# Reordering the stages of a diffusion trunk: the first gate products and all chunk inverses go ahead of the query pass, and those gates' weights are split by ScalarE and GpSimd

## The chip, the cores and the metric

The kernel runs on one core of a Trainium2 chip. The metric is device time in microseconds (us) of one execution. Engines are named as the profile names them: PE (TensorE matmul), DVE (VectorE), ACT (ScalarE), POOL (GpSimd), SP (SyncE, which here issues most DMAs).

## The reference

One layer of a trunk over 2048 latent tokens and 256 context tokens, model width 1024. The tokens are normalised and modulated (`h`), and one wide input projection feeds two mixers and their gates:

```
qkv, beta, decay, k_att, v_att = split(h @ w_state)
za, q_att, zb, ga, gb          = split(h @ w_rest)
q, k, v = l2norm/silu(short_conv5(qkv))             # 4 heads of 128
oa = delta_rule(q, k, v, g, beta)  +  the same backwards in time
ob = windowed attention(q_att, k_att, v_att, sink)   # 8 heads of 64
y  = sigmoid(ga) * (norm(oa)*silu(za) @ w_proj_a) + sigmoid(gb) * (ob*silu(zb) @ w_proj_b)
out = x + gate * (y @ w_out)
```

The delta rule runs in chunks. For each chunk, head and direction a unit lower triangular matrix is inverted, `t_mat = solve(I + a_mat)`, where `a_mat` is made of that chunk's keys, decays and betas alone; queries don't enter it. The inverses are then used by a scan over the chunks, which carries a state forwards and one backwards, and which needs the queries for its outputs. The gate products `za, zb, ga, gb` (3072 columns) depend on `h` alone.

## The kernel before

All matrices are fp32, and each large product is made of three: an operand is split into a high part rounded to fp32r and a low part (`wh`, `wl` for weights, `hh`, `hl` for the tokens), and high x high, low x high and high x low are summed. So each block of weights first costs two elementwise steps: a rounding copy (`wh <- wr`, L242, on POOL) and a subtraction (`wl <- wr, wh`, L243, on DVE), both in `weights` at L235. `fm_dense` (L520) then makes 24 products of 128 x 512 for each 128 columns and each group of 512 tokens.

The stages, in the order in which the program is written:

1. Modulation, normalised tokens `hh0..hh3` (four groups of 512 tokens) and the context `hh4`, attention keys and values.
2. Keys and values of the delta rule (`qkv(ORDER, ...)`, L678): products `lps`, copied to a tile `y` by ACT (L633), a convolution over five tokens on DVE (L562, L564), transposes and chunk products on PE (`zt` L594, `gps` L603 and L617), and the results stored to DRAM: the chunk matrices to `Nsp`, the betas to `brT` (L543, in `scalars2`).
3. The query pass (L700): `qkv([0, 1, 2, 3])` for the delta rule's queries, and between its groups `q_block` for the attention's queries (products `tmps`, 256 columns wide, L365 to L367).
4. The first gates (L837): all 24 blocks of 128 gate columns for token groups 2 and 3 (`rps`, 1152 products), each followed by a tanh on ACT (L809) and, for the first 8 blocks, a DVE product (L811). Beside them runs `mod_gate`, whose sums `gacc` are made on POOL (L223).
5. The inverses. `base` (L719) inverts 128 triangular matrices at once, one to a partition, by 62 steps of two DVE products each (L746, L748); it is called for two sets of chunks. `base4` (L763) does the last 32 matrices, each spread over four partitions: it reloads `N` from `Nsp`, scales it (L778, L779), copies it to the other partitions by DMA (L783), makes 63 pairs of products (L788, L790) and stores `X4sp` by 16 DMAs (L795).
6. The scan, with the gates of groups 1 and 0 between its steps; then attention, output projections, and the last product.

The scheduler of the framework reorders instructions of each engine within the bounds of their dependences, by a priority that follows the written order; what results is shown below where it matters. On one engine instructions then run strictly in that order, and an instruction that waits holds up all behind it.

Memory is taken from pools. A pool that is opened after another was closed on the same side gets the same SBUF addresses, and its tiles wait, tile by tile, for the last use of what lay there. Before, the pools of stages 2 and 3 for `y`, `cacc` and their like (`p1y`, `p1b`) are one pair that stays open through both; they are closed before the gates, and `base2` (which holds the second set's `N`, and `btmp`, `nb` and the tiles of `base4`) is opened in their place. It stays open to the end of the scan. Of the sum buffers that `lps`, `tmps` and `rps` share (`acc`), there are three.

Of the kernel before, what the change touches and what calls it, by code (L numbers as in the profile page):

```python
# [7 lines left out]
F32 = mybir.dt.float32  # L8
F32R = mybir.dt.float32r
BF16 = mybir.dt.bfloat16  # L10
AF = mybir.ActivationFunctionType
ALU = mybir.AluOpType
# [5 lines left out]
KT = D // 128  # L18
NB, NCB = L // 128, LC // 128
NC = NB + NCB  # L20
H = 4
EPS = 1e-6
C_ST, C_QB = 1536, 2320
# [5 lines left out]
def f32(ap):  # L29
    return ap.bitcast(F32)  # L30
# [10 lines left out]
def _hybrid(ctx, tc, nc, V, S, G, T, ins, out, dbg, upto):  # L41
    dma = nc.sync.dma_start
# [8 lines left out]
    def mem(tag):  # L51
        if dbg is not None:
            print("MEM", tag, tile.free_sbuf_bytes_per_partition(tc))
# [11 lines left out]
    w_in = ins["w_in"][0]  # L65
# [166 lines left out]
            dma(gsp[:, n * 512:n * 512 + 512], grow)  # L232
            yield

    def weights(src, kt):  # L235

        wh = wq.tile([128, KT, 128], F32R, name="wh")
        wl = wq.tile([128, KT, 128], F32R, name="wl")
        for k in range(0, kt, 4):
            wr = wq.tile([128, 4, 128], F32, name="wr", bufs=2)  # L240
            dma(wr, src[k * 128:(k + 4) * 128].rearrange("(k p) c -> p k c", p=128))
            G.tensor_scalar(wh[:, k:k + 4], wr, 1.0, 1.0, op0=ALU.mult, op1=ALU.mult)  # L242
            V.tensor_tensor(wl[:, k:k + 4], wr, f32(wh[:, k:k + 4]), op=ALU.subtract)  # L243
        return wh, wl

    ORDER = [8, 9, 10, 11, 4, 5, 6, 7]
# [2 lines left out]
    if True:  # L249
# [48 lines left out]
        for j in range(2):  # L298
            mps = [psum("acc" if n == 0 else "hps", [4, 512], name=f"mps{n}") for n in range(2)]
            for k in range(KT):  # L300
# [10 lines left out]
                if j == 0 and 2 <= k < 2 + NCB:  # L311
                    c = k - 2
# [48 lines left out]
        def tm_dense(c, wh, wl, n):  # L361
            ps = acc([128, 512], name="tmps")
            xh, xl = hsrc(c)
            for k in range(KT):
                T.matmul(ps[:, :n], lhsT=xh[:, k], rhs=wh[:, k], start=k == 0, stop=False)  # L365
                T.matmul(ps[:, :n], lhsT=xl[:, k], rhs=wh[:, k], start=False, stop=False)
                T.matmul(ps[:, :n], lhsT=xh[:, k], rhs=wl[:, k], start=False, stop=k == KT - 1)  # L367
            return ps[:, :n]

        with tc.issue_after(wm_dma.ins):  # L370
            wh, wl = tm_weights(C_ST, NST)
# [4 lines left out]
        def norm_w(pool, nm):  # L376

            wn = pool.tile([128, 2, 64], F32, name="wn", bufs=1)
            with tc.issue_after(wm_dma.ins):
                dma(wn[:, 0], ins[nm].to_broadcast([128, 64]))  # L380
            x, y = (wn[:, j].rearrange("p (a h f) -> p a h f", a=2, h=2) for j in range(2))
            G.tensor_copy(y[:, :, 0], x[:, :, 1])
            G.tensor_copy(y[:, :, 1], x[:, :, 0])
            return wn

        wn = norm_w(pa, "k_norm_w")
# [81 lines left out]
        def q_block(pool, c, hv, ps, wn):  # L468
            y = qk_norm_rope(pool, 2, ps, 4, c, wn)
            qh = pb.tile([128, 4, 2, 64], F32R, name="qh", tag="st")  # L470
            S.copy(qh[:, :, 0], y)
            V.tensor_tensor(qh[:, :, 1], y, f32(qh[:, :, 0]), op=ALU.subtract)
            kt = psum("zt", [128, 4, 128], F32R)
            for h in range(4):
                T.transpose(kt[:, h], qh[:, h].rearrange("p x d -> p (x d)"), identr)
            qs = pb.tile([128, 4, 128], F32, name="qs", tag="o")
            S.copy(qs, f32(kt))
            adma(Qsp[c - NCB, :, hv * 4:hv * 4 + 4], qs)
# [3 lines left out]
        for gi in range(8):  # L482
            xts = []
            for j in range(2):
                c = NCB + gi * 2 + j
# [5 lines left out]
            if gi == 7:  # L491
                px_.__exit__(None, None, None)
                wq_ = tc.tile_pool(name="wts", bufs=2, reuse_waits="tile")
                wq = wq_.__enter__()
            c = NCB + gi * 2
# [125 lines left out]

    def qkv(order, after, w=None, beside=()):
        w = w or weights(w_in[:, order[0] * 128:order[0] * 128 + 128], KT)
        beside = iter(beside)
        for mi, m in enumerate(order):
            segs = [(hh[4], hl[4], 0, LC)] if m >= 4 else []
            segs += [(hh[gi], hl[gi], NCB + gi * 4, 512) for gi in range(4)]
            ys = []
            for si, (xh, xl, c0, n) in enumerate(segs):
                ps = acc([128, 512], name="lps")[:, :n]  # L630
                fm_dense(ps, w, xh, xl)
                y = py.tile([128, 516], F32, name="y", bufs=4)
                S.copy(y[:, 2:2 + n], ps)  # L633
                if c0 <= NCB:
                    V.memset(y[:, 0:2], 0.0)
                else:
                    V.tensor_copy(y[:, 0:2], ys[-1][0][:, 512:514])
                    V.tensor_copy(ys[-1][0][:, 514:516], y[:, 2:4])
                if c0 == 0 or c0 == NCB + 12:
                    V.memset(y[:, n + 2:n + 4], 0.0)  # L640
                ys.append((y, c0, n))
                if si == 1:
                    nxt = order[mi + 1] if mi + 1 < len(order) else after
                    wnext = None if nxt is None else weights(w_in[:, nxt * 128:nxt * 128 + 128], KT)
                if si == len(segs) - 1:
                    w = wnext
                    done = [ys[-2], ys[-1]]
                elif c0 > NCB or c0 == 0:
                    done = [ys[-1 if c0 == 0 else -2]]
                else:  # L650
                    done = []
                for y_, c_, n_ in done:
                    finish(m, conv(y_, m, n_), c_, n_)
                next(beside, None)
            if 4 <= m < 8:
                sk = ssk[:, :, m % 4]
                G.tensor_scalar(sk, sk, 4 * EPS, 1.0, op0=ALU.add, op1=ALU.mult)
                V.reciprocal(rk2[:, :, m % 4], sk)
                rsq(rin[:, :, m % 4], sk, 1)
            if m < 4:  # L660
                aq = alpha[:, :, m]
                G.tensor_scalar(aq, aq, 4 * EPS, 1.0, op0=ALU.add, op1=ALU.mult)
                rsq(aq, aq)
                G.tensor_scalar(aq, aq, 0.5 * 128 ** -0.5, 1.0, op0=ALU.mult, op1=ALU.mult)
# [16 lines left out]
    dc_.__exit__(None, None, None)  # L681
    hpools.pop().__exit__(None, None, None)

    def q_pass(pool):
        wn = norm_w(pool, "q_norm_w")
        for hv in range(2):
            wh = pool.tile([128, KT, 256], F32R, name="qwh", bufs=1)
            wl = pool.tile([128, KT, 256], F32R, name="qwl", bufs=1)
            col = C_QB + hv * 256
            for k in range(0, KT, 2):  # L690
                wr = wq.tile([128, 2, 256], F32, name="wrq", tag="wr")
                dma(wr, w_in[k * 128:(k + 2) * 128, col:col + 256].rearrange("(k p) c -> p k c", p=128))
                G.tensor_scalar(wh[:, k:k + 2], wr, 1.0, 1.0, op0=ALU.mult, op1=ALU.mult)
                V.tensor_tensor(wl[:, k:k + 2], wr, f32(wh[:, k:k + 2]), op=ALU.subtract)
            for c in range(NCB, NC):
                q_block(pool, c, hv, tm_dense(c, wh, wl, 256), wn)
                if c % 2 == 1:
                    yield

    with tc.tile_pool(name="q_pass", bufs=2, side="right", reuse_waits="tile") as pq:  # L700
        jobs = q_pass(pq)
        qkv([0, 1, 2, 3], None, None, jobs)
        for _ in jobs:
            pass
    bs_ = tc.tile_pool(name="base", bufs=1, side="right", reuse_waits="tile")
    bs = bs_.__enter__()

# [86 lines left out]
                    p0 = q * 32 + d * 16 + ci * 8  # L794
                    dma(X4sp[d, ci, q], X[p0:p0 + 8])  # L795

    def rest(ev, m, groups):

        col, dst, mm = ((C_ZA, zasp, m) if m < 4 else (C_ZB, zbsp, m - 4) if m < 8 else
                        (C_GA, gasp, m - 8) if m < 16 else (C_GB, gbsp, m - 16))  # L800
        w = weights(w_in[:, col + mm * 128:col + mm * 128 + 128], KT)
        return w, dst, mm

    def rest_run(ev, job, m, gi):
# [10 lines left out]
    PACE = -1  # L815
    NWO = 5
    LAT = lambda *cs: [NCB + c for c in cs]
    mem("p1b q")
    pb_.__exit__(None, None, None)
    py_.__exit__(None, None, None)  # L820
    psum_phase("right", mg0=1, mg1=1, og=1, gd0=1, gd1=1)

    def gates(ms, gis, beside=()):
        beside = iter(beside)
        job = rest(ev, ms[0], None)
        for i, m in enumerate(ms):
            for j, gi in enumerate(gis):
                rest_run(ev, job, m, gi)
                if j == 0:
                    nxt = rest(ev, ms[i + 1], None) if i + 1 < len(ms) else None  # L830
                    next(beside, None)
            job = nxt

    bs2_ = tc.tile_pool(name="base2", bufs=1, reuse_waits="tile")
    bs2 = bs2_.__enter__()
    with tc.tile_pool(name="gate", bufs=1, reuse_waits="tile") as gp:
        gates(list(range(24)), (2, 3), mod_gate(gp, ones))  # L837
    LAST = (LAT(14, 15), LAT(0, 1))
    for si, (fr, bk, np_) in enumerate((([0, 1] + LAT(*range(0, 6)), [0, 1] + LAT(*range(10, 16)), bs),
                                        (LAT(*range(6, 14)), LAT(*range(2, 10)), bs2))):  # L840
# [2 lines left out]
                pass  # L843
    base4(*LAST)
    mem("r1a")
    bs_.__exit__(None, None, None)
    hpools.pop().__exit__(None, None, None)
    hpools.pop().__exit__(None, None, None)

# [292 lines left out]
    with tc.tile_pool(name="scan", bufs=1, side="right", reuse_waits="tile") as scp:  # L1142
# [6 lines left out]
        gates(list(range(4, BESIDE)), (1, 0))  # L1149
        mem("r1b")  # L1150
        scl_.__exit__(None, None, None)
    bs2_.__exit__(None, None, None)


    def proj_w():
# [193 lines left out]
```

## Time and profile before

| | us |
|---|---|
| three runs | 2044.96, 2047.9, 2050.6 (median 2047.9) |
| the profiled execution | 2046.15 |
| its span, first to last instruction | 2044.3 |
| PE busy in the span | 1966.8 (96%) |
| DVE busy | 1421.5 (70%) |
| ACT busy | 760.4 (37%) |
| POOL busy | 742.9 (36%) |

Times in a trace are us from the start of the span. Matmuls overlap their neighbours, so a matmul is listed with 0.40 us and yet starts 0.23 us after the one before it; idle PE in a window is its length less the busy time. `PEclk` is the share of the full clock that PE was granted. In a row of instruction groups stand the line, the engine, the operation, output and inputs, their sizes, the count, the total busy time, the mean in ns, and the idle time of the engine before them with what ended it.

### The profile page before, as it was taken

How to read it: one execution, taken by the hardware profiler on the slowest of the kernel's cores; microseconds unless marked ns; L12 is line 12 of the kernel's file. 1: busy time of each engine (PE TensorE's matmuls, PEld its weight loads, DVE VectorE, ACT ScalarE, POOL GpSimd, SP SyncE). 2: the span in 40 equal slices, each digit the busy share in tenths (PEclk: the TensorE clock that was granted, in tenths of full speed). 3: DMA queues.
4: the chain of work that ended last, by engine and by line, in shares of the span. 5: the costliest groups of instructions: out<-in, count | busy, mean ns of one | idle time of the engine just before them, and what ended most of it. 6: DMA issues, size and time to landing. Idle time of an engine off the chain costs nothing. (4 is left out here: it accounts for less than half of the span.)

```text
span 2044.3 us, 32068 instructions
## 1 busy us (share of the span) xinstructions
PE 1966.8 (96%) x11043; PEld 1643.2 (80%) x11043; DVE 1421.5 (70%) x2715; ACT 760.4 (37%) x1927; POOL 742.9 (36%) x876
## 2 busy tenths in 40 slices
PE   6899999989999999999999999999989999999999
PEld 3888888778898677787788888878868888878887
DVE  6888766667766999999689655536577777753322
ACT  5655555544443211101122233325476556531100
POOL 2862211235553433224322234324256443442321
PEclk8999999999999999999999999999999999999999
DMA  7462236754447533437876787663456655355542
GB/s 256 141 166 85 89 97 165 188 149 155 147 136 197 154 109 111 132 98 220 201 218 205 221 244 214 185 207 116 129 165 204 185 167 158 120 174 189 185 144 93
DMA packets 375511, 333.12 MB, mean 163 GB/s; under 512 B 83832, under 2 KB 299184, under 8 KB 374708
## 3 DMA queue, kind: packets, MB, share of 16 engines
q1 hardware_dynamic: 347924, 288.59, 49.1%
q10 hardware_dynamic: 27424, 42.48, 5.9%
q8 instruction: 87, 1.43, 0.3%
q14 instruction: 76, 0.62, 0.1%
HBM read 220.28 MB, written 109.13 MB: 161 GB/s over the span
## 5 line engine op out<-in xcount | busy, mean ns | idle before, releaser
L523 PE MATMUL rps<-hh,wh 128*128 128x512 f32 x768 | 309.9, 404 | 10.1 <-DVE rt L811 5.2
L525 PE MATMUL rps<-hh,wl 128*128 128x512 f32 x768 | 310.3, 404 | 1.6 <-DVE wl L243 1.6
L524 PE MATMUL rps<-hl,wh 128*128 128x512 f32 x768 | 307.8, 401 | 0.0
L242 POOL TENSOR_SCALAR wh<-wr 128x512 fp32r<-128x512 f32 x120 | 104.7, 885 | 278.6 <-PE rps L524 105.8
L523 PEld LDWEIGHTS rps<-hh,wh 128*128 128x128 f32 x768 | 145.6, 190 | 47.1 <-POOL wh L242 4.9
L525 PEld LDWEIGHTS rps<-hh,wl 128*128 128x128 f32 x768 | 145.4, 189 | 35.1 <-DVE wl L243 2.4
L523 PE MATMUL lps<-hh,wh 128*128 128x512 f32 (+1 forms) x448 | 172.1, 384 | 0.3 <-ACT y L633 0.3
L524 PEld LDWEIGHTS rps<-hl,wh 128*128 128x128 f32 x768 | 145.8, 190 | 32.9
L525 PE MATMUL lps<-hh,wl 128*128 128x512 f32 (+1 forms) x448 | 171.1, 382 | 0.0
L524 PE MATMUL lps<-hl,wh 128*128 128x512 f32 (+1 forms) x448 | 171.1, 382 | 0.0
L562 DVE SCALAR_TENSOR_TENSOR cacc<-y,cw,cacc 128x512 f32<-128x512 f32 (+1 forms) x224 | 160.6, 739 | 14.3 <-ACT cacc L560 11.3
L809 ACT ACTIVATE rt<-rps 128x512 f32<-128x512 f32 x96 | 57.3, 597 | 287.5 <-PE rps L525 228.6
L909 DVE CUSTOM_DVE_ANT_0 pr<-sc,band,sk 128x640 f32<-128x640 f32 (+1 forms) x128 | 106.4, 863 | 42.5 <-PE sc L905 22.1
L937 DVE TENSOR_TENSOR pl<-pt,ph 128x512 fp32r<-128x512 f32 x156 | 105.0, 685 | 40.9 <-ACT ph L935 40.3
L935 ACT CAST ph<-pt 128x512 fp32r<-128x512 f32 x156 | 90.2, 585 | 111.7 <-PE pt L933 77.0
L748 DVE TENSOR_TENSOR N<-N,btmp 128x62 f32<-128x62 f32 (+30 forms) x124 | 123.7, 997 | 3.1
L746 DVE TENSOR_TENSOR btmp<-N 128x62 f32<-128x62 f32 (+30 forms) x124 | 119.2, 962 | 3.2
L919 POOL TENSOR_SCALAR pr<-pr,sm 128x640 f32<-128x640 f32 (+1 forms) x128 | 98.9, 793 | 57.1 <-DVE sm L917 44.5
L911 ACT ACTIVATE pr<-pr,sm 128x640 f32<-128x640 f32 (+1 forms) x128 | 104.0, 815 | 24.6 <-DVE sm L909 24.6
L1198 PE MATMUL pps<-yh,wph 128*128 128x512 f32 x256 | 105.1, 414 | 5.0 <-DVE tb L1206 2.0
L243 DVE TENSOR_TENSOR wl<-wr,wh 128x512 fp32r<-128x512 f32 x120 | 94.0, 796 | 18.1 <-POOL wh L242 17.9
L1199 PE MATMUL pps<-yl,wph 128*128 128x512 f32 x256 | 101.7, 397 | 0.9 <-DVE yl L1181 0.9
(301 smaller groups left out, 4925.9 us busy)
## 6 DMA issues: line engine op xcount, KB each, us to landing
wr<-in_w_in_dram SPq DMA_DIRECT2D x120, 256.0 KB
kw<-Ksp SPq DMA_DIRECT2D x28, 384.0 KB
x<-vsp SPq DMA_DIRECT2D x36, 256.0 KB
k<-ksp SPq DMA_DIRECT2D x34, 256.0 KB
kT<-kTsp SPq DMA_DIRECT2D x34, 256.0 KB
wm<-in_w_mod_dram SPq DMA_DIRECT2D x16, 512.0 KB
xt<-in_x_dram SPq DMA_DIRECT2D x16, 512.0 KB
dtl<-Dsp SPq DMA_DIRECT2D x32, 256.0 KB
```

Source lines behind the costliest of these rows:

```text
L242: G.tensor_scalar(wh[:, k:k + 4], wr, 1.0, 1.0, op0=ALU.mult, op1=ALU.mult)
L523: T.matmul(ps, lhsT=wh[:, k], rhs=xh[:, k], start=k == 0, stop=False)
L524: T.matmul(ps, lhsT=wh[:, k], rhs=xl[:, k], start=False, stop=False)
L525: T.matmul(ps, lhsT=wl[:, k], rhs=xh[:, k], start=False, stop=k == kt - 1)
L562: V.scalar_tensor_tensor(a, y[:, t:t + n], cw[:, m, t:t + 1], a, op0=ALU.mult, op1=ALU.add)
L746: V.tensor_tensor(tv, A[:, m + 1:, m].unsqueeze(2).to_broadcast([h1 + n, r, m]), A[:, m, 0:m].unsqueeze(1).to_broadcast([h1 + n, r, m]), o ...
L748: V.tensor_tensor(A[:, m + 1:, 0:m], A[:, m + 1:, 0:m], tv, op=ALU.add)
L909: V.tensor_tensor_reduce(s_, ps[:, o:768], band[:, b0:b0 + W + 256], -0.125, sk[:, 1, hd:hd + 1], ALU.add, ALU.min, sm[:, h, 1:2])
L911: S.activation(s_, s_, AF.Exp, scale=-1.0, bias=sm[:, h, 1:2], accum_out=sm[:, h, 2:3])
L937: V.tensor_tensor(pl, pt, f32(ph), op=ALU.subtract)
L1198: T.matmul(ps, lhsT=wh[:, k, ms], rhs=hs[k], start=k == 0, stop=False)
L1199: T.matmul(ps, lhsT=wh[:, k, ms], rhs=ls[k], start=False, stop=False)
```

## The change

Stage 4 and all of stage 5 move ahead of stage 3: keys and values, then gates and inverses, then the query pass, then the scan. For these gates alone the weights are split by ACT (the rounding copy, `S.copy`) and POOL (the subtraction) in place of POOL and DVE. Pools and banks follow: `p1y` and `p1b` are closed after the keys and values, `base2` takes their place; it is closed when the inverses are written down, and a second pair `q1y`, `q1b` is opened at the same addresses for the query pass. Lines of the changed kernel are numbered otherwise: the subtraction for these gates is L244, base's products L729 and L731, base4's L771 and L773, its scaling L761 and L762, its stores L778, the copy to `y` L637.

```diff
-    def weights(src, kt):
+    def weights(src, kt, beside_base=False):
...
-            G.tensor_scalar(wh[:, k:k + 4], wr, 1.0, 1.0, op0=ALU.mult, op1=ALU.mult)
-            V.tensor_tensor(wl[:, k:k + 4], wr, f32(wh[:, k:k + 4]), op=ALU.subtract)
+            if beside_base:
+                S.copy(wh[:, k:k + 4], wr)
+                G.tensor_tensor(wl[:, k:k + 4], wr, f32(wh[:, k:k + 4]), op=ALU.subtract)
+            else:
+                G.tensor_scalar(wh[:, k:k + 4], wr, 1.0, 1.0, op0=ALU.mult, op1=ALU.mult)
+                V.tensor_tensor(wl[:, k:k + 4], wr, f32(wh[:, k:k + 4]), op=ALU.subtract)
...
-    def q_pass(pool):
...
-    with tc.tile_pool(name="q_pass", bufs=2, side="right", reuse_waits="tile") as pq:
-        jobs = q_pass(pq)
-        qkv([0, 1, 2, 3], None, None, jobs)
-        for _ in jobs:
-            pass
     bs_ = tc.tile_pool(name="base", bufs=1, side="right", reuse_waits="tile")
...
-    psum_phase("right", mg0=1, mg1=1, og=1, gd0=1, gd1=1)
+    psum_phase("right")
+    psum_phase("right", gd0=1, gd1=1)
...
-        gates(list(range(24)), (2, 3), mod_gate(gp, ones))
+        gates(list(range(24)), (2, 3), mod_gate(gp, ones), True)
...
     base4(*LAST)
     mem("r1a")
+    bs2_.__exit__(None, None, None)
     bs_.__exit__(None, None, None)
+
+    def q_pass(pool):
...
+    psum_phase("right")
+    psum_phase("right", zt=3, gps=2)
+    py_ = tc.tile_pool(name="q1y", bufs=2, reuse_waits="tile")
+    py = py_.__enter__()
+    pb_ = tc.tile_pool(name="q1b", bufs=2, reuse_waits="tile")
+    pb = pb_.__enter__()
+    with tc.tile_pool(name="q_pass", bufs=2, side="right", reuse_waits="tile") as pq:
+        jobs = q_pass(pq)
+        qkv([0, 1, 2, 3], None, None, jobs)
+        for _ in jobs:
+            pass
...
+    psum_phase("right", mg0=1, mg1=1, og=1, gd0=1, gd1=1)
     hpools.pop().__exit__(None, None, None)
     hpools.pop().__exit__(None, None, None)
...
         scl_.__exit__(None, None, None)
-    bs2_.__exit__(None, None, None)
```

What this makes of the order on two engines. First DVE around `base4`, whose pairs of products write `btmp`. Before, these are its rows a little after the pairs begin; the names other than `N` and `btmp` are the scan's and the gates' (in brackets stand the semaphores that a row waits for; DMAHW are those of DMAs):

```order
L788 TENSOR_TENSOR btmp<-N,btmp 128x61 [waits DVE_49]
L790 TENSOR_TENSOR btmp<-btmp 128x61 [waits DVE_49]
L1120 TENSOR_TENSOR oa_10579<-ops,oa_10579 128x512 [waits PE_49]
L788 TENSOR_TENSOR btmp<-N,btmp 128x60 [waits DVE_49]
L1076 TENSOR_TENSOR v_10609<-vps,brs 128x512 [waits PE_49]
L790 TENSOR_TENSOR btmp<-btmp 128x60 [waits DVE_49]
L1076 TENSOR_TENSOR v_10647<-vps,brs 128x512 [waits PE_49]
L788 TENSOR_TENSOR btmp<-N,btmp 128x118 [waits DVE_49]
L243 TENSOR_TENSOR wl<-wr,wh 128x512 [waits DMAHW3_49,PE_49,Pool_49]
```

In the changed kernel the pairs of `base4` stand in one block of 126 rows with nothing between them. This is the block's end and what follows it, the first `y` of the query pass:

```order
L771 TENSOR_TENSOR btmp<-N,btmp 128x32 [waits DVE_49]
L773 TENSOR_TENSOR btmp<-btmp 128x32 [waits DVE_49]
L771 TENSOR_TENSOR btmp<-N,btmp 128x16 [waits DVE_49]
L773 TENSOR_TENSOR btmp<-btmp 128x16 [waits DVE_49]
L639 MEMSET y 128x2 [waits DMAHW4_49,DMAHW3_49,DMAHW5_49,DMAHW2_49,DMAHW6_49,DMAHW1_49,DMAHW7_49,DMAHW0_49,DVE_49]
L641 COPY y<-y 128x2 [waits Activation_49]
L476 TENSOR_TENSOR qh<-xn,qh 128x4x64 [waits Activation_49] x2
L402 TENSOR_TENSOR xn<-tmps,ssn 128x256 [waits DVE_49,PE_49]
```

`base4` stood among the scan's work before and now stands alone between the second set of inverses and the query pass, whose first memset of `y` waits for DVE itself and for all eight DMA semaphores.

Second ACT at the head of the query pass. Before, with the tail of the keys and values (`junk`, `st`, `pt`) around the first `sq` and `y` of the queries:

```order
L392 ACTIVATE sq<-tmps 128x256 [waits PE_49]
L560 ACTIVATE cacc<-y,cw 128x512 [waits DMAHW6_49]
L600 ACTIVATE junk,ssk<-zt 128x128 [waits PE_49,Activation_49]
L600 ACTIVATE junk,ssk<-zt 128x128 [waits Activation_49] x2
L633 COPY y<-lps 128x512 [waits DVE_49,PE_49]
L600 ACTIVATE junk,ssk<-zt 128x128 [waits Activation_49]
L612 COPY st<-zt 128x512 [waits DMAHW4_49]
```

In the changed kernel, from the last tanh of the gates (`rt`) on:

```order
L792 ACTIVATE rt<-rps 128x512 [waits DMAHW2_49,PE_49]
L795 DMA gbsp_132<-rt 128x512 [waits Activation_49]
L396 ACTIVATE sq<-tmps 128x256 [waits PE_49]
L396 ACTIVATE sq<-tmps 128x256 [waits DVE_49,PE_49] x2
L637 COPY y<-lps 128x512 [waits DMAHW3_49,DMAHW4_49,DMAHW2_49,DMAHW5_49,DMAHW1_49,DMAHW6_49,DMAHW0_49,DMAHW7_49,DVE_49,Pool_49]
L475 CAST qh<-xn 128x4x64 x2
L637 COPY y<-lps 128x512
L564 ACTIVATE cacc<-y,cw 128x512 [waits DVE_49,Activation_49] x2
```

The copy of the first `lps` to `y` waited for PE and DVE. Now PE is covered by the `sq` ahead of it, and the copy waits for DVE, for POOL and for DMAs on all eight semaphores. The DMAs that stand last in those eight, in SP's order, are the second eight stores of `X4sp` (L778).

More of the change, by code (lines that the diff above doesn't have):

```diff
@@ L682, in _hybrid @@
     hpools.pop().__exit__(None, None, None)
-    def q_pass(pool):
[L685 to L698, printed above, removed]
-    with tc.tile_pool(name="q_pass", bufs=2, side="right", reuse_waits="tile") as pq:
-        jobs = q_pass(pq)
-        qkv([0, 1, 2, 3], None, None, jobs)
-        for _ in jobs:
-            pass
     bs_ = tc.tile_pool(name="base", bufs=1, side="right", reuse_waits="tile")
@@ L795, in base4, with rest @@
                     dma(X4sp[d, ci, q], X[p0:p0 + 8])
-    def rest(ev, m, groups):
+    def rest(ev, m, beside_base):
         col, dst, mm = ((C_ZA, zasp, m) if m < 4 else (C_ZB, zbsp, m - 4) if m < 8 else
                         (C_GA, gasp, m - 8) if m < 16 else (C_GB, gbsp, m - 16))
-        w = weights(w_in[:, col + mm * 128:col + mm * 128 + 128], KT)
+        w = weights(w_in[:, col + mm * 128:col + mm * 128 + 128], KT, beside_base)
         return w, dst, mm
@@ L817, in _hybrid, with gates @@
     LAT = lambda *cs: [NCB + c for c in cs]
-    mem("p1b q")
     pb_.__exit__(None, None, None)
     py_.__exit__(None, None, None)
-    psum_phase("right", mg0=1, mg1=1, og=1, gd0=1, gd1=1)
-    def gates(ms, gis, beside=()):
+    psum_phase("right")
+    psum_phase("right", gd0=1, gd1=1)
+    def gates(ms, gis, beside=(), beside_base=False):
         beside = iter(beside)
-        job = rest(ev, ms[0], None)
+        job = rest(ev, ms[0], beside_base)
         for i, m in enumerate(ms):
@@ L829, in gates @@
                 if j == 0:
-                    nxt = rest(ev, ms[i + 1], None) if i + 1 < len(ms) else None
+                    nxt = rest(ev, ms[i + 1], beside_base) if i + 1 < len(ms) else None
                     next(beside, None)
@@ L845, in _hybrid @@
     mem("r1a")
+    bs2_.__exit__(None, None, None)
     bs_.__exit__(None, None, None)
+    def q_pass(pool):
+        wn = norm_w(pool, "q_norm_w")
+        for hv in range(2):
+            wh = pool.tile([128, KT, 256], F32R, name="qwh", bufs=1)
+            wl = pool.tile([128, KT, 256], F32R, name="qwl", bufs=1)
+            col = C_QB + hv * 256
+            for k in range(0, KT, 2):
+                wr = wq.tile([128, 2, 256], F32, name="wrq", tag="wr")
+                dma(wr, w_in[k * 128:(k + 2) * 128, col:col + 256].rearrange("(k p) c -> p k c", p=128))
+                G.tensor_scalar(wh[:, k:k + 2], wr, 1.0, 1.0, op0=ALU.mult, op1=ALU.mult)
+                V.tensor_tensor(wl[:, k:k + 2], wr, f32(wh[:, k:k + 2]), op=ALU.subtract)
+            for c in range(NCB, NC):
+                q_block(pool, c, hv, tm_dense(c, wh, wl, 256), wn)
+                if c % 2 == 1:
+                    yield
+    psum_phase("right")
[9 more added lines that the diff above has]
+            pass
+    mem("p1b q")
+    pb_.__exit__(None, None, None)
+    py_.__exit__(None, None, None)
+    psum_phase("right")
+    psum_phase("right", mg0=1, mg1=1, og=1, gd0=1, gd1=1)
     hpools.pop().__exit__(None, None, None)
```

## The prediction

> **What bounds the kernel now.** I read the page's slices first, then windows of one slice each around the two stages that change places, then the groups of instructions, and last the timeline of DVE and SP at the ends of the inverses.
>
> ```profile
> PE   6899999989999999999999999999989999999999
> DVE  6888766667766999999689655536577777753322
> ...
> 358.00:409.00 51.00, 46.29 (x269) 38.45 (x267) 33.49 (x66) 25.99 (x84) 12.57 (x14) 1.00 0.74 187
> 409.00:460.00 51.00, 42.89 (x275) 38.13 (x276) 32.97 (x70) 24.24 (x81) 18.04 (x21) 0.93 0.57 149
> 460.00:511.00 51.00, 49.48 (x356) 45.54 (x355) 36.28 (x81) 22.48 (x68) 25.60 (x37) 1.00 0.50 154
> ...
> 664.00:715.00 51.00, 45.91 (x185) 35.20 (x184) 47.56 (x58) 10.61 (x17) 21.04 (x17) 0.97 0.57 156
> ...
> 766.00:818.00 52.00, 49.02 (x203) 38.77 (x202) 50.93 (x49) 7.51 (x13) 18.65 (x15) 0.97 0.36 111
> ...
> 869.00:920.00 51.00, 51.00 (x219) 41.03 (x219) 49.72 (x47) 5.04 (x9) 13.63 (x10) 1.00 0.35 98
> 920.00:971.00 51.00, 48.47 (x284) 39.02 (x282) 48.98 (x68) 7.26 (x15) 22.47 (x24) 0.97 0.75 221
> 971.00:1022.00 51.00, 47.82 (x311) 40.46 (x311) 32.58 (x63) 7.85 (x20) 16.90 (x21) 0.97 0.82 201
> 1022.00:1073.00 51.00, 48.23 (x356) 42.48 (x355) 45.39 (x113) 11.73 (x37) 13.45 (x19) 0.97 0.76 219
> ```
>
> The columns are PE, its weight loads, DVE, ACT and POOL, then PE's clock and the DMA share. PE is the bound nearly everywhere: a window without idle time holds 219 products, 51/219 = 0.233 us each. In the gates (664 to 945) DVE is full as well, and PE only just gets its weights. So the change can win no more than what PE loses in these windows. Idle time in the eight windows that aren't full: 4.7 + 8.1 + 1.5 (into the query pass), 5.1 + 3.0 (gates), 2.5 + 3.2 + 2.8 (start of the scan, with the rest of the inverses on DVE) = 30.9 us. Lost clock, length by (1 - PEclk): 0.07 x 51 = 3.6 and five times about 1.5 = 7.7, together 11. **All that can be won: 42 us.**
>
> **What it moves onto PE's path.** Before, `base4` runs on DVE while PE works on the scan. In the changed order it stands alone, and the first copy of the query pass into `y` waits for it to its last store: `base2` is closed, `q1y` takes its addresses, and the first `y` lies on `btmp`. There are three sum buffers. PE makes one `lps` and two `tmps` of the query pass, then one `lps` and one `tmps` more in the two buffers that DVE empties; the next `tmps` needs the buffer of the first `lps`, and that is emptied by the waiting copy. PE is strictly in order, so it stands. How long is the time from when PE runs dry to when `X4sp` has landed.
>
> **When PE runs dry.** The order is that of before up to the end of the keys' and values' `lps`, where before the first `tmps` starts:
>
> ```profile
> 381.23 1.06 PE L603 MATMUL gps<-cacc 128*128 128x128 f32 x8
> ...
> 401.16 0.28 PE L365 MATMUL tmps<-qwh,hh 128*128 128x256 f32 x1
> 401.28 0.28 PE L366 MATMUL tmps<-qwh,hl 128*128 128x256 f32 x1
> ```
>
> From there 1152 gate products at 0.234 = 270 us, the 78 small products left of the keys and values at 1.06/8 = 0.13 or less, 10, and 48 `lps` at 0.234 with 72 `tmps` at 0.12, together 20. 401 + 270 + 10 + 20 = **701**, if nothing stalls. A stall of the gates on the way comes off the wait behind it and doesn't change the sum.
>
> **When the inverses start.** They need `brT`.
>
> ```profile
> 445.62 0.94 SPq L543 DMA_DIRECT2D brT<-bt  x2
> ...
> 646.98 0.47 SPq L733 DMA_DIRECT2D N<-Nsp  x1
> ...
> 658.83 1.90 DVE L738 TENSOR_TENSOR N<-N,nb 64x256 f32<-64x256 f32 x3 [4.36 <-DMA N<-Nsp]
> ...
> 662.92 0.26 DVE L746 TENSOR_TENSOR btmp<-N 128x62 f32<-128x62 f32 x1
> 663.21 0.28 DVE L748 TENSOR_TENSOR N<-N,btmp 128x62 f32<-128x62 f32 x1
> ...
> 980.60 0.22 DVE L748 TENSOR_TENSOR N<-N,btmp 128x62 f32<-128x62 f32 x1
> 981.53 0.11 DVE L755 MEMSET N<- 128x64 f32 x1 [0.71 <-POOL btmp L772]
> ```
>
> In the new order 134 gate products and some 60 small ones stand ahead of the transposes for `brT`: 401 + 31 + 8 = 440, against 445.6 before. Then 5 for copy, issue and landing (2 to 8), the load of `N` as before (646.98 to 658.83, 12) and the scaling (4): the first pair at **461** (455 to 470).
>
> **How long the pairs take.**
>
> ```profile
> L748 DVE TENSOR_TENSOR N<-N,btmp 128x62 f32<-128x62 f32 (+30 forms) x124 | 123.7, 997 | 3.1
> L746 DVE TENSOR_TENSOR btmp<-N 128x62 f32<-128x62 f32 (+30 forms) x124 | 119.2, 962 | 3.2
> L243 DVE TENSOR_TENSOR wl<-wr,wh 128x512 fp32r<-128x512 f32 x120 | 94.0, 796 | 18.1 <-POOL wh L242 17.9
> L811 DVE SCALAR_TENSOR_TENSOR rt<-rt,rps 128x512 f32<-128x512 f32 x32 | 21.7, 680 | 1.9 <-ACT rt L809 1.7
> L223 POOL TENSOR_TENSOR gacc<-gacc,wmg 128x512 f32<-128x512 f32 x14 | 23.6, 1689 | 28.6 <-ACT wmg L221 26.3 <-DVE N L748 2.2
> L1166 POOL TENSOR_TENSOR wpl<-wpr,wph 128x512 fp32r<-128x512 f32 x16 | 20.6, 1294 | 10.8 <-ACT wph L1165 9.8 <-DMA wpr<-in_w_proj_b_dram 1.0
> ...
> 684.60 1.27 POOL L223 TENSOR_TENSOR gacc<-gacc,wmg 128x512 f32<-128x512 f32 x1 [0.42 <-ACT wmg L221]
> ...
> 684.65 1.64 DVE L748 TENSOR_TENSOR N<-N,btmp 128x392 f32<-128x392 f32 x1
> ...
> 833.70 0.57 DVE L748 TENSOR_TENSOR N<-N,btmp 128x392 f32<-128x392 f32 x1
> ```
>
> The 248 products take 123.7 + 119.2 = 243 us, and the row after 662.92 starts 0.03 behind its end: 248 x 0.03 = 8. Of other work on DVE, by rows and order, remain the second set's scaling (7), 8 products of the gates (0.68 each, 5), 8 weight subtractions of the query pass (0.8, 6) and its first blocks (9): 27. The 48 subtractions of the gates' weights, 38 us at 0.796, are gone from DVE: that is the gain of the split. But POOL now makes them, at the 1.29 of its like (L1166), and the last rows show what that does to DVE: the same product of 128x392 takes 0.57 alone and 1.64 beside a POOL addition, 1.07 more. By 461 about (461 - 401 - 10)/0.234 = 214 gate products are done, four or five blocks of 48, and the weights run two ahead, so 36 of the 48 fall on the pairs. Between nothing and 1.07 each (0 to 39 us) I take 0.7, near the upper row since DVE then runs little else: 25. Pairs end at 461 + 243 + 8 + 27 + 25 = **764**.
>
> The Trainium skill, page "SBUF — State Buffer", section "Who interferes with whom", speaks against this half of the change: a DVE instruction with two SBUF inputs and a GpSimd one that reads SBUF lock each other out, and the second to come waits for the whole first. By it DVE could lose all of the 1.29, 36 x 1.29 = 46 in place of 25, and the forecast would be 21 higher; the 1.07 of 1.27 above nearly agrees.
>
> **From there to the first `y`.**
>
> ```profile
> 983.15 1.12 SPq L758 DMA_DIRECT2D Xsp<-N  x2
> ...
> 995.34 0.79 SPq L776 DMA_DIRECT2D N<-Nsp  x2
> ...
> 1003.53 4.41 DVE L778 TENSOR_TENSOR N<-N,btmp 32x4096 f32<-32x4096 f32 x1 [11.25 <-DMA x<-vsp]
> 1011.13 4.41 DVE L779 TENSOR_TENSOR N<-N,nb 32x4096 f32<-32x4096 f32 x1
> ...
> 1026.43 0.26 DVE L788 TENSOR_TENSOR btmp<-N,btmp 128x63 f32<-128x63 f32 x1 [5.53 <-DMA N<-N]
> ...
> L790 DVE TENSOR_TENSOR btmp<-btmp 128x252 f32<-128x252 f32 (+52 forms) x63 | 27.8, 441 | 1.2
> L788 DVE TENSOR_TENSOR btmp<-N,btmp 128x252 f32<-128x252 f32 (+52 forms) x63 | 24.8, 393 | 6.6 <-DMA N<-N 5.5
> ...
> 1173.29 1.11 SPq L795 DMA_DIRECT2D X4sp<-btmp  x3
> ```
>
> Last memset and issue 2; the inverses' 2 MB must land before `N` is loaded anew, at the 200 GB/s of these windows 10 (3 to 12); the load 1003.5 - 995.3 = 8; two scalings 9; copies to the other partitions, 1026.4 - 1015.5 = 11, less beside idle queues, 10; 126 products 52.6, with 4 for their starts, 57, less where POOL is quiet, 53 (49 to 57); 16 stores at 1.11/3 = 0.37, 6, and a landing of 2 to 3. Together 101 (88 to 110). `y` is free at **865**, and PE has stood 865 - 701 = **164 us**.
>
> **The sum.** 164 lost; 6 for the start behind it (the clock falls after idle stretches, above, and the first convolution has to come through; 3 to 12); 42 won, since neither the old entry to the query pass nor the inverses beside gates and scan hold PE up any more (half of that at worst). The query pass itself stays bound by PE: in 460:511 DVE has 36 of 51 us. The other stages issue what they issued. 164 + 6 - 42 = **+128 us**. The profiled execution took 2046.15, 1.75 under the median of 2047.9: 2174 there, **2176** against the median. With all bounds on one side, the low sum is 128 - 6 - 25 - 13 - 3 = 81 us (2129), the high one 128 + 9 + 14 + 9 + 6 + 21 = 187 (2235). The range is 2125 to 2225.
>
> **Rivals.**
> - *The inverses are through before PE runs dry.* Then only the 42 us count: 2048 - 42 = 2006. For it: 38 us leave DVE. It decides where `y` is free by 701, so the pairs would have to start and end within 701 - 101 - 461 = 139 us; the rows give 243 for the products alone. 2%.
> - *PE waits for the second set alone*, because the tile that the first copy needs isn't one of `base4`'s. `y` is then free at 764: 63 + 6 - 42 = +27, 2075. Against it: the copy waits for all eight DMA semaphores, which the last stores hold. 5%.
> - *POOL holds DVE up for whole instructions, and DVE holds POOL up.* POOL's masks of the inverses (`affine_select`) stand between the weights and wait for DVE. That stretches the gates, which is covered by the wait, but each lost us of DVE comes off the end: +21 by POOL's full 1.29, and as much again if chains of waits form: 2197 to 2240. 18%.
>
> The forecast has 73%; 2% are left for what I don't see. A difference under 0.3% (6 us) can't be told from none here. Faster by more than that: the first rival and a little, 0.03; the same 0.01; slower 0.96.
>
> **What would show it.** Right: one stretch in which PE is idle for 100 us or more between the gates and the query pass, PE's wait put down to the copy into `y` or to the stores of `X4sp`; DVE with nothing but L771 and L773 for its last 50 us; pairs (L729, L731) that take 10 to 40 us more than 243 in total; no idle PE left at the scan's start. Wrong: `tmps` and convolutions running between `base4`'s products, or PE windows without idle time through the query pass; then a buffer came free that I hold to be taken. If the stretch is there and the total is far off, a term of the 865 is.

## The result, and the profile after

The changed kernel takes 2180.1 us (median of five runs, 2173.7 to 2182.3) where the kernel before takes 2047.9 (2045.0 to 2050.6): 1.0645 times as long, 95% interval 1.0629 to 1.0661. The profiled execution has a span of 2176.7 us, 132.4 more than before.

These are the slices of the page, 54 us each, as before in tenths; the last row is the clock that PE was granted:

```profile
PE   6899999989898501999999999999999999999999
DVE  6888766659999847676545555643558777753322
PEclk8999999999999855999999999999999999999999
```

Two slices of PE are all but empty, and the one ahead of them is half full. What PE waited for, over the whole run (total, times, longest):

```profile
PE tmps L369 <- ACT y L637: 115.6, 1, 115.6
PE rps L529 <- POOL wl L244: 11.2, 2, 6.2
PE lps L527 <- DVE xn L402: 10.2, 1, 10.2
PE rps L527 <- DVE rt L794: 9.8, 3, 8.0
```

One wait of 115.6 us stands for the copy into `y`. The other three come to 31.2; they lie ahead of it, in the gates and at the first products of the query pass. The windows around the stop, and two from the start of the scan (PE, weight loads, DVE, ACT, POOL, clock, DMA share):

```profile
715.00:766.00 51.00, 22.09 (x116) 18.33 (x114) 43.75 (x59) 1.15 (x3) 16.04 (x17) 0.78 0.18 49
766.00:818.00 52.00, 0.00 (x0) 0.00 (x0) 21.74 (x45) 0.00 (x0) 1.95 (x7) 0.50 0.40 81
818.00:869.00 51.00, 4.26 (x20) 4.26 (x21) 39.58 (x108) 2.92 (x6) 1.08 (x1) 0.50 0.07 16
869.00:920.00 51.00, 51.00 (x352) 46.51 (x352) 34.31 (x80) 22.72 (x68) 24.92 (x33) 0.99 0.47 145
...
1073.00:1124.00 51.00, 51.00 (x297) 41.55 (x296) 19.62 (x35) 8.50 (x18) 16.75 (x21) 1.00 0.78 235
1124.00:1175.00 51.00, 51.00 (x385) 44.35 (x384) 26.78 (x66) 11.58 (x32) 12.82 (x18) 1.00 0.64 182
```

Even DVE is idle for more than half of 766 to 818: there the chain goes through DMAs. DVE's timeline shows its steps, and ACT's where it ends:

```profile
464.09 3.04 DVE L721 TENSOR_TENSOR N<-N,nb 64x256 f32<-64x256 f32 x4 [4.26 <-DMA N<-Nsp]
...
471.34 0.25 DVE L729 TENSOR_TENSOR btmp<-N 128x62 f32<-128x62 f32 x1
...
770.58 0.11 DVE L738 MEMSET N<- 128x64 f32 x1 [0.71 <-POOL btmp L755]
789.26 4.41 DVE L761 TENSOR_TENSOR N<-N,btmp 32x4096 f32<-32x4096 f32 x1 [18.57 <-DMA N<-Nsp]
...
807.62 0.26 DVE L771 TENSOR_TENSOR btmp<-N,btmp 128x63 f32<-128x63 f32 x1 [9.50 <-DMA N<-N]
...
856.47 0.17 DVE L773 TENSOR_TENSOR btmp<-btmp 128x16 f32<-128x16 f32 x1
864.18 0.06 DVE L639 MEMSET y<- 128x2 f32 x1 [7.53 <-DMA X4sp<-btmp]
```

```profile
864.10 0.59 ACT L637 COPY y<-lps 128x512 f32<-128x512 f32 x1 [114.50 <-DMA X4sp<-btmp]
```

PE's last product ahead of the stop starts at 748.91, and the next one at 864.74; 48 products `lps` and 72 `tmps` stand between the gates and the stop, as the prediction had counted from the three sum buffers. Both engines that fill `y` name the stores of `X4sp` as what they waited for. The groups that the forecast of the pairs rests on:

```profile
L729 DVE TENSOR_TENSOR btmp<-N 128x62 f32<-128x62 f32 (+30 forms) x124 | 133.1, 1073 | 3.7
L731 DVE TENSOR_TENSOR N<-N,btmp 128x62 f32<-128x62 f32 (+30 forms) x124 | 131.5, 1060 | 3.7
L244 POOL TENSOR_TENSOR wl<-wr,wh 128x512 fp32r<-128x512 f32 x48 | 80.3, 1689 | 131.9 <-ACT wh L243 119.1 <-DMA wr<-in_w_in_dram 12.7
```

The products of the pairs take 264.6 us in place of 243, and a POOL subtraction takes 1.69 in place of the 1.29 of its like.

### The profile page after: what moved, and what is told of

The parts are those of the page before. It is cut to its first block, busy times and chain, and to the rows that moved or that the text cites. A ratio compares the mean times of both kernels' runs of the same rounds, so it can differ in the third digit from the quotient of the medians.

```text
span 2176.7 us, 32093 instructions
## 1 busy us (share of the span) xinstructions
PE 1965.3 (90%) x11043; PEld 1640.3 (75%) x11043; DVE 1414.8 (65%) x2667; ACT 788.3 (36%) x1975; POOL 766.7 (35%) x876
## 4 chain that ended last, share of the span: by engine, by line
PE 63%; DVE 18%; DMA 8%; POOL 3%; issue 2%; SPq 2%; ACT 2%; DVEq 0%; ACTq 0%; POOLq 0%
DVE btmp L729 5%; DVE N L731 5%; PE rps L527 4%; PE rps L529 4%; PE rps L528 4%; PE lps L527 4%; PE lps L528 3%; PE lps L529 3%; PE ops L1300 3%; PE ops L1302 3%; PE ops L1301 3%; PE pps L1215 2%; PE pt L951 2%; PE pps L1216 2%; PE pps L1217 2%
## 5 line engine op out<-in xcount | busy, mean ns | idle before, releaser
L369 PE MATMUL tmps<-qwh,hh 128*128 128x256 f32 x256 | 73.7, 288 | 117.1 <-ACT y L637 115.6
L369 PEld LDWEIGHTS tmps<-qwh,hh 128*128 128x128 f32 x256 | 49.1, 192 | 118.3 <-ACT y L637 115.8
L729 DVE TENSOR_TENSOR btmp<-N 128x62 f32<-128x62 f32 (+30 forms) x124 | 133.1, 1073 | 3.7
L731 DVE TENSOR_TENSOR N<-N,btmp 128x62 f32<-128x62 f32 (+30 forms) x124 | 131.5, 1060 | 3.7
L244 POOL TENSOR_TENSOR wl<-wr,wh 128x512 fp32r<-128x512 f32 x48 | 80.3, 1689 | 131.9 <-ACT wh L243 119.1
```

Source lines behind the costliest of these rows:

```text
L729: V.tensor_tensor(tv, A[:, m + 1:, m].unsqueeze(2).to_broadcast([h1 + n, r, m]), A[:, m, 0:m].unsqueeze(1).to_broadcast([h1 + n, r, m]), o ...
L731: V.tensor_tensor(A[:, m + 1:, 0:m], A[:, m + 1:, 0:m], tv, op=ALU.add)
```

## The experiments

The theory to test: PE stops because the first `y` of the query pass lies on memory of `base2` and so waits for `base4`'s last store. The rivals: DVE's work by itself is what PE waits for; the new split is what costs; the order itself costs, whatever the memory. Ratios are against the kernel before, run on the same chip beside each experiment, with 95% intervals.

**no_pairs.** The changed kernel, and in `base4`:

```diff
-        for m in range(63):
-            ...
-            V.tensor_tensor(X[:, m + 1:, 0:n], X[:, m + 1:, 0:n], tv, op=ALU.add)
```

> The changed kernel without base4's 63 pairs of products; its load, scaling, copies and stores stay (32 of the inverses are then not computed). Theory of the memory: the first y of the query pass waits for base4's stores, whatever DVE does meanwhile. The pairs held DVE from 801 to 856, so y comes 55 us earlier, at about 810, and PE stands for about 60 us, most of that with DVE idle: 2125 us. Rival, DVE's work is what PE waits for: with the pairs gone DVE is free when the second set is done, at 771, and PE waits only some 25 us: about 2090 us.

Measured: 2122.7 us, ratio 1.0381 [1.0359, 1.0403]. The waits and DVE's timeline of this run:

```profile
PE tmps L369 <- ACT y L637: 47.5, 1, 47.5
...
PE zt L479 <- DVE qh L476: 10.4, 2, 9.4
```

```profile
770.63 0.11 DVE L738 MEMSET N<- 128x64 f32 x1 [0.71 <-POOL btmp L755]
791.57 4.41 DVE L761 TENSOR_TENSOR N<-N,btmp 32x4096 f32<-32x4096 f32 x1 [20.82 <-DMA X4sp<-btmp]
...
800.38 0.06 DVE L639 MEMSET y<- 128x2 f32 x1
809.92 0.17 DVE L641 COPY y<-y 128x2 f32<-128x2 f32 x1 [9.49 <-DMA N<-N]
```

The waits shrink to 47.5 and 9.4, about the 60 of the theory. (The first `y` comes at 796, behind the first scaling of `N`, since the stores have no products to wait for; the second comes at 810, behind the copies of `N`. In the changed kernel the pairs hold DVE from 807.6, not from 801 as I had written.) They don't vanish: DVE works 9 us between 771 and 810 and is idle for 30, and PE stands all the same, for transfers out of and into the old tiles. So DVE's work alone is not the answer.

**base4_behind.** The changed kernel with

```diff
-    base4(*LAST)
     mem("r1a")
     bs2_.__exit__(None, None, None)
...
     psum_phase("right", mg0=1, mg1=1, og=1, gd0=1, gd1=1)
+    bs2_ = tc.tile_pool(name="base3", bufs=1, reuse_waits="tile")
+    bs2 = bs2_.__enter__()
+    base4(*LAST)
```

> base4 is written behind the query pass, in a pool of its own at the same addresses; all else as in the changed kernel. Theory of the memory: the first y now waits for the second set alone (last product at 771, its stores at 783 at the latest), so PE stands for 24 to 36 us in place of 116, and base4 runs beside the scan as before, which costs up to 5: 2090 to 2105 us. Rival, the sum of DVE's work sets the time wherever base4 stands: it comes back as waits of PE in the scan, and the time stays above 2130. Rival, the split is what costs: 2180 less a few.

Measured: 2097.8 us, ratio 1.0253 [1.0237, 1.0269].

```profile
PE tmps L369 <- ACT y L637: 21.4, 1, 21.4
...
PE zt L479 <- DVE qh L476: 9.1, 2, 8.1
```

Some 80 us of the loss are gone with `base4`'s place alone, at the same addresses and with the same work in all. What is left of the stop (21.4 and 8.1) is the wait for the second set: for its last product until 770.5, then for its stores until 782.8.

**old_split and split_only.** The first is the changed order with the old split, the second the old order with the new split:

```diff
-        gates(list(range(24)), (2, 3), mod_gate(gp, ones), True)
+        gates(list(range(24)), (2, 3), mod_gate(gp, ones), False)
```

> The changed order, with the first gates' weights split as before by POOL (rounding copy) and DVE (subtraction). Theory of the memory, with the prediction's sizes: some 36 subtractions of 0.8 us come back onto DVE ahead of the inverses' end (+29), the 22 us that POOL's subtractions cost the pairs go: stop and time 7 longer, 2180 to 2195. Rival, the split is what costs: the 22 us and PE's 11 us of waiting for wl go and the subtractions fit between: 2145 to 2160.

> The kernel before with nothing changed but the split of the first gates' weights (ScalarE and POOL). Theory of the memory: DVE loses 36 subtractions (29) and gains some 20 by POOL's reads beside it, PE waits for DVE in that stage for 8 us only: 2040 to 2050 us. Rival, the split is what costs: slower by 15 to 35, 2063 to 2083.

Measured: old_split 2170.1 us, 1.0607 [1.0584, 1.0629]; split_only 2068.8 us, 1.0113 [1.0096, 1.0131]. Both go against the sizes that I had put on the split: it costs 23 us in the old order, as the rival had it, and in the new one some 10, between the two forecasts (the intervals of old_split and of the changed kernel just touch). Groups of old_split, then waits and groups of split_only:

```profile
L731 DVE TENSOR_TENSOR N<-N,btmp 128x62 f32<-128x62 f32 (+30 forms) x124 | 116.2, 937 | 3.3
L729 DVE TENSOR_TENSOR btmp<-N 128x62 f32<-128x62 f32 (+30 forms) x124 | 114.4, 922 | 3.4
```

```profile
PE rps L527 <- DVE rt L815: 11.9, 8, 6.5
PE rps L529 <- POOL wl L244: 6.6, 3, 4.3
```

```profile
L752 DVE TENSOR_TENSOR N<-N,btmp 128x62 f32<-128x62 f32 (+30 forms) x124 | 137.1, 1105 | 3.9
L750 DVE TENSOR_TENSOR btmp<-N 128x62 f32<-128x62 f32 (+30 forms) x124 | 133.1, 1073 | 3.8
L244 POOL TENSOR_TENSOR wl<-wr,wh 128x512 fp32r<-128x512 f32 x48 | 88.6, 1863 | 65.1 <-ACT wh L243 52.3 <-DMA wr<-in_w_in_dram 12.8
```

With the old split the pairs take 230.6 us, 34 less than the 264.6 of the changed kernel; with the new one in the old order, 270.2. There PE has no long stop to hide it, and waits for the gates' weights and for DVE's product on `rt`, which stands among the longer pairs: from 640 to 1000 us PE is idle for 31.0 us, in the kernel before for 10.6. These runs don't say yet whether POOL's subtraction or ScalarE's copy is to blame.

**act_dve and before_act.** ScalarE still rounds, but DVE subtracts, in the new order and in the old:

```diff
                 S.copy(wh[:, k:k + 4], wr)
-                G.tensor_tensor(wl[:, k:k + 4], wr, f32(wh[:, k:k + 4]), op=ALU.subtract)
+                V.tensor_tensor(wl[:, k:k + 4], wr, f32(wh[:, k:k + 4]), op=ALU.subtract)
```

> The changed order; the first gates' weights rounded by ScalarE and subtracted by DVE, so that POOL does neither. Theory of the contention (a POOL subtraction holds up the DVE product that runs beside it; ScalarE's copies cost nothing): the pairs fall from 265 to 230 us as with the old split, or lower by what POOL's rounding copies cost there, at most 48 x 0.4 = 19; the 36 subtractions come back (+29); y free at 845 to 858 and 2160 to 2172 us. Rival, ScalarE's copies wait for weights in front of the tanh and so hold up PE and DVE: pairs as before, but later, y free after 864, 2180 or more.

> The kernel before, with the rounding copies of the first gates' weights on ScalarE in place of POOL; the subtractions stay on DVE. split_only lost 23 us with this and the subtraction on POOL. Theory of the contention: it was POOL's subtraction; this one is 2040 to 2052 us, pairs 230 to 243. Rival, it was ScalarE, whose copies wait for the weights in front of the tanh that PE waits for: 2058 to 2070, with PE waiting for rt as in split_only.

Measured: act_dve 2165.1 us, 1.0578 [1.0557, 1.0599], below the changed kernel without overlap; before_act 2036.9 us, 0.9952 [0.9933, 0.9971], **half a per cent faster than the kernel before**, and better than its forecast of 2040 to 2052. Groups of act_dve, then of before_act:

```profile
L729 DVE TENSOR_TENSOR btmp<-N 128x62 f32<-128x62 f32 (+30 forms) x124 | 112.9, 910 | 3.4
L731 DVE TENSOR_TENSOR N<-N,btmp 128x62 f32<-128x62 f32 (+30 forms) x124 | 111.5, 900 | 3.2
```

```profile
L750 DVE TENSOR_TENSOR btmp<-N 128x62 f32<-128x62 f32 (+30 forms) x124 | 117.2, 945 | 3.2
L752 DVE TENSOR_TENSOR N<-N,btmp 128x62 f32<-128x62 f32 (+30 forms) x124 | 115.3, 930 | 3.1
...
L244 DVE TENSOR_TENSOR wl<-wr,wh 128x512 fp32r<-128x512 f32 x48 | 34.3, 732 | 3.4 <-ACT wh L243 3.4
```

It is POOL's subtraction: act_dve differs from the changed kernel, and before_act from split_only, in nothing else. With ScalarE's copies and without it the pairs take 224.4 (new order) and 232.5 us (old, 243 before), and DVE waits for a rounded weight for 13.3 us in the new order and 3.4 in the old. The rival that ScalarE's copies hold up the tanh is out: PE's wait for DVE's product on `rt` falls from 9.8 to 4.7 us in the new order and from 11.9 to 5.7 in the old.

In the changed order the split works through the moment at which `y` comes free. The first copy into `y` starts at 864.1 in the changed kernel, at 856.0 in old_split and at 853.2 in act_dve (forecast 845 to 858), though PE's stop is longer in the last two (130.8 and 134.2 us). From there to the end of the run are 1312.6, 1313.1 and 1309.8 us. Counted from the end of the last wait for the old tiles it is 1309.5 in no_pairs (809.9) and 1313.1 in base4_behind (782.8). So in all five runs the total is the time at which the memory comes free, plus the same rest within 4 us.

**act_scan.** before_act with the same split for the gates beside the scan:

```diff
-        gates(list(range(4)), (1, 0))
+        gates(list(range(4)), (1, 0), (), True)
...
-        gates(list(range(4, BESIDE)), (1, 0))
+        gates(list(range(4, BESIDE)), (1, 0), (), True)
```

> before_act with ScalarE rounding the weights of the gates beside the scan as well (15 blocks for groups 1 and 0). Theory of the contention: POOL's one-input copies cost DVE little (6 us over 48 beside the pairs), and beside the scan DVE has room, so this is the same as before_act within 5: 2032 to 2042 us. Rival, ScalarE stands between the scan's steps and waits for DVE and PE there, so that a copy behind it comes late: 2045 to 2060.

Measured: 2033.2 us, 0.9931 [0.9909, 0.9953]; from before_act it can't be told apart. Both beat the kernel before and the changed one, the kernel before by less than 1%.

**set2_behind, set2_behind_old, set2_behind_act.** The order with the memory out of the way, and its three splits (as in the changed kernel, in old_split and in act_dve). The edit, with `base_set(si, pool)` for the loop's body:

```diff
-    for si, (fr, bk, np_) in enumerate(...):
-        ...
-    base4(*LAST)
+    base_set(0, bs)
...
     psum_phase("right", mg0=1, mg1=1, og=1, gd0=1, gd1=1)
+    bs2_ = tc.tile_pool(name="base3", bufs=1, reuse_waits="tile")
+    bs2 = bs2_.__enter__()
+    base_set(1, bs2)
+    base4(*LAST)
```

> The changed order with only the first set of inverses beside the gates; the second set and base4 are written behind the query pass, in a pool opened after it. Theory of the memory: PE stands nowhere for a tile of the second set or of base4, the first set is done at about 630, well ahead of the query pass at 720; but the whole second set (130 us of DVE) now lies beside the start of the scan, where before its last half cost PE 8 us in three windows. base4_behind's 2098 less its waits of 22 and 8, plus 8 to 25: 2075 to 2095. Rival, the order itself is what costs, since DVE's work all has to be done by the scan's first steps: over 2100.

> As set2_behind, with the old split (POOL copy, DVE subtraction). Theory of the contention: the split costs in this order what it costs in the order of before, some 10 to 23: 2055 to 2080. If the memory was the whole trouble of the order, this comes to the time before, 2046, or to a few us below. Rival, the order itself costs: over 2085.

> As set2_behind, but the first gates' weights rounded by ScalarE and subtracted by DVE, the split that made before_act the fastest. Theory: the split and the order add up. The ScalarE split was worth 9 us in the order of before and 5 in the changed order (2165 against 2170 with the old split), so 2059 to 2064 us. Rival, the order itself costs nothing once the memory is out of the way, and the remaining 23 us of set2_behind_old came from the gates: 2030 to 2045.

Measured: 2079.9 us, 1.0166 [1.0148, 1.0184]; 2068.8, 1.0109 [1.0094, 1.0124]; 2063.0, 1.0079 [1.0058, 1.0101], each within its forecast. The splits rank as before: POOL's subtraction costs some 17 us against the best one. But with any split the order is slower than its twin in the old order, by 26 us with the best (2063.0 against 2036.9), though PE stands nowhere for `y`. So the changed kernel's distance to before_act, 143 us, falls into four steps: 82 for `base4`'s place, 18 for the second set's, 17 for POOL's subtraction, and 26 that stay with the order. The longest waits of set2_behind_act:

```profile
PE sc L926 <- DMA qT<-Qsp: 12.6, 1, 12.6
PE fps L1061 <- DVE oa L1054: 5.2, 1, 5.2
```

Both are at the end of the scan and the start of the attention behind it, around 1430.

**only_set2_behind.** To see why, `base4` goes back ahead of the query pass:

```diff
     base_set(0, bs)
+    base4(*LAST)
...
     base_set(1, bs2)
-    base4(*LAST)
```

> As set2_behind_act, but base4 stays ahead of the query pass and only the second set is written behind it. The pairs of the first set (464 to 617) and base4 (some 86 from load to last store) end at about 710, when PE needs the first y (710 to 720), so PE should not stand there. It asks where set2_behind_act loses its 26 us against before_act: up to 1226 it lies 16 us ahead in PE's lost time, and from 1329 to 1482 it falls 40 behind. Theory, base4's lateness (its last pair at 1330, before at 1133) keeps the scan's last chunks waiting: this one is 2020 to 2040 us. Rival, the scan waits for the second set at 970 and 1175, the scheduler fills that time with gate products, and these are missing at the scan's end: 2055 to 2065.

Measured: 2063.4 us, 1.0077 [1.0052, 1.0102], the same as set2_behind_act. So `base4`'s lateness isn't it, and the number is the rival's. That the gate products are used up early shows in how many of them (`rps`) PE does in two windows of before_act, then of this run:

```profile
1100.00:1200.00 100.00, 40.13 (x146) 25.88 (x146) 1.17 (x2) 3.60 (x6) 1.00 0.78 225
1300.00:1400.00 100.00, 71.68 (x289) 53.03 (x290) 0.00 (x0) 7.16 (x12) 1.00 0.52 163
```

```profile
1100.00:1200.00 100.00, 75.97 (x293) 55.18 (x294) 0.00 (x0) 7.45 (x13) 0.97 0.60 170
1300.00:1400.00 100.00, 44.01 (x157) 28.46 (x158) 0.00 (x0) 3.98 (x7) 0.97 0.70 200
```

The numbers change places: 293 gate products while the second set is being finished (its last pair starts at 1170, in before_act at 967), where before_act does 146, and 157 against 289 from 1300 to 1400. The loss itself lies in the 100 us behind these, here for all of PE's work, in before_act and then in this run:

```profile
1400.00:1500.00 100.00, 95.80 (x509) 79.11 (x507) 59.39 (x128) 53.91 (x116) 40.16 (x45) 1.00 0.46 138
```

```profile
1400.00:1500.00 100.00, 78.24 (x396) 63.60 (x395) 57.07 (x125) 49.12 (x121) 39.32 (x49) 0.90 0.55 170
```

PE does 17.6 us less, at a clock of 0.90 in place of 1.00 (up to 10 us more). The attention starts there at 1445, behind a wait of 13.2 us for its first queries, whose load SP issues only at 1438; from 1450 to 1500 PE has no gate product left. In before_act the attention starts at 1359, and 69 gate products still stand between 1450 and 1500. That fits a store of work that covers waits once only. That giving these products back, or loading the queries earlier, would win the 26 us was not tried and stays an inference.

## Why the prediction was right, point by point

- **What bounds the kernel, and the stop.** Right. PE stands once, 115.6 us, for a `y` that waits for the stores of `X4sp`; base4_behind takes some 80 us of the loss away by moving `base4` alone, and no_pairs shows the wait going on with DVE idle.
- **PE runs dry at 701 if nothing stalls.** PE stopped behind 748.9. Take off the waits of 31.2 and 718 remain. Of the 17 us between, the granted clock explains some 12: it is 0.90, 0.93 and 0.93 in the windows from 460, 562 and 664, 51 x (0.10 + 0.07 + 0.07). I had charged no lost clock to the gates. As forecast, none of this reaches the sum, since it comes off the wait behind it: 115.6 + 31.2 + 17 = 164.

```profile
460.00:511.00 51.00, 42.20 (x170) 33.24 (x169) 41.71 (x50) 12.29 (x20) 18.55 (x14) 0.90 0.61 155
...
562.00:613.00 51.00, 45.99 (x187) 36.66 (x188) 49.80 (x36) 9.65 (x17) 24.29 (x13) 0.93 0.34 99
...
664.00:715.00 51.00, 44.82 (x183) 35.64 (x182) 49.90 (x40) 7.08 (x12) 18.43 (x11) 0.93 0.24 73
```

- **First pair at 461 (455 to 470).** Wrong by 10 us, outside its bounds: 471.3. The loads of the first set's `N` were taken to land together as before, but the second direction's were scaled from 464.1 only, with a wait for `N<-Nsp` ahead, and on DVE two scalings of the second set then came in front of the first pair, behind 2.55 us of idle time.
- **The pairs end at 764.** Measured 770, of which the late start is 10; from first pair to end it is 298.6 against 303 forecast, and the products 264.6 against 243 + 25 = 268.
- **The split is a gain (38 us off DVE for 25 of contention).** This step failed. The 243 us were taken for the products' price in quiet, but POOL's work lay in them as well: with the subtractions back on DVE they take 230.6 (POOL copies) or 224.4 (ScalarE copies). So POOL's 36 subtractions beside the pairs (36 of 48 start behind 471, as forecast) cost 264.6 - 224.4 = 40 us, 1.1 each in place of 0.7, and what they replace is 36 x 0.8 = 29: a loss of 11, and act_dve's `y` is free 10.9 earlier. The total hid this by luck, because 243 + 25 and 224 + 40 come to nearly the same sum. The Trainium skill ("SBUF — State Buffer", section "Who interferes with whom") has a DVE instruction with two SBUF inputs and a GpSimd one that reads SBUF lock each other out. An estimate by that rule, POOL's whole 1.29 for each of the 36, is 46; the measured 40 lies between my 25 and it.
- **From there to the first `y`, 101 us.** Measured 94 from the last pair's end at 769.9 to ACT's copy at 864.1: the pairs of `base4` took 49.0 in place of 53 (807.6 to 856.6, at the lower bound), what lies ahead of them 37.7 in place of 39 (2 + 10 + 8 + 9 + 10), and the stores 7.5 in place of 8 to 9. `y` was free at 864 against 865: by luck, errors of +10, -4 and -7 cancelled.
- **6 lost at the start behind it, 42 won.** Before, 2044.3 - 401.2 = 1643 us follow the first `tmps`, and PE does 300 of them ahead of the stop; so 1343 + 6 - 42 = 1307 were to be left at 864.7. Measured are 2176.7 - 864.7 = 1312, a net gain of 31 in place of 36; no run splits it into its two terms. The windows at the start of the scan hold no idle PE now.
- **The rivals.** The first fell with the 299 us that the pairs need from end to end. The second (PE waits for the second set alone) was made true in base4_behind: 2097.8 in place of its 2075. Its 764 was the pairs' end alone; the second `y` also waited for the second set's stores, until 782.8, which makes 19 of the 23 us. The third has its mechanism confirmed, in that POOL and DVE do hold each other up for nearly whole instructions, but not its total.

## What to carry to other kernels

A stage moved ahead is not only its instructions: look up which tiles' addresses the next stage takes over, and what must land before they come free; a chain that ran hidden beside other work stands bare once the next stage waits for its memory. Work that is moved to an idle engine isn't free if the two engines hold each other up, as POOL's subtraction and DVE's products did here: price it by the busy engine's longer instructions, and take their price in quiet from a run without the neighbour, not from a mean that already holds some of it. Here the rounding copy belonged on ScalarE and the subtraction back on DVE, and the old order with that split is the fastest of those measured.

## What the runs showed of the hardware

DVE and POOL nearly took turns, and both paid for it. These are rows of the changed kernel, first DVE, then POOL, and the same DVE product with no POOL work beside it in act_dve:

```profile
564.32 2.13 DVE L729 TENSOR_TENSOR btmp<-N 128x990 f32<-128x990 f32 x1
...
566.48 2.13 DVE L731 TENSOR_TENSOR N<-N,btmp 128x990 f32<-128x990 f32 x1
```

```profile
565.37 2.20 POOL L244 TENSOR_TENSOR wl<-wr,wh 128x512 fp32r<-128x512 f32 x1
```

```profile
561.47 1.19 DVE L729 TENSOR_TENSOR btmp<-N 128x990 f32<-128x990 f32 x1
```

1.19 us become 2.13, and POOL's 1.29 become 2.20. One DVE product starts 2.16 us after the other; one product and one subtraction strictly in turn would take 1.19 + 1.29 = 2.48. POOL's one-input rounding copies cost far less: over the pairs 230.6 - 224.4 = 6 us in the new order, 242.9 - 232.5 = 10 in the old. And the clock granted to PE, 0.50 in the windows without work, was back at 0.99 in the window from 869 on, some 5 us after the first product: until 869.2 the `tmps` start 0.21 us apart, ahead of the stop 0.11.
